# Second product of each attention score over 128 rows instead of 64, in a two-layer hybrid encoder

## The chip, the cores and the metric

The kernel runs on one core of a Trainium2 chip. The metric is device time in microseconds (us) of one execution; less is better. The engines of the core are PE (TensorE, the matrix engine; PEld is its loading of stationary operands), DVE (VectorE), ACT (ScalarE), POOL (GpSimd) and SP (SyncE, which here only issues transfers). They run unsynchronised, each through its own list of instructions, and wait for each other by semaphores.

## The reference

Two layers over 256 tokens of width 1024, in float32. Cut to what matters:

```python
h = rmsnorm(x, n1)
qa, ka, va, qb, kb, vb = jnp.split(h @ w_in, cuts, axis=-1)
ya = global_gqa(axial_rope(rmsnorm(qa)), axial_rope(rmsnorm(ka)), va)   # 8 heads, 2 k/v heads
yb = dilated_window_attention(partial_rope(qb), partial_rope(kb), vb)   # 8 heads
y = jnp.concatenate([rmsnorm(ya, out_norm_a), rmsnorm(yb, out_norm_b)], axis=-1)
x = x + y @ w_out
u = jnp.square(jax.nn.relu(rmsnorm(x, n2) @ w_mlp_in))
x = x + u @ w_mlp_out
```

Each of the 16 heads of a layer has 64 dimensions, so a score is a product over 64 rows: `s = q . k` for 256 queries and 256 keys, then a softmax and a product with v.

## The kernel before, in words

Every float32 operand of a product is held as two parts, hi (rounded to the type fp32r in which PE takes it) and lo (the rest), and a product is hi·hi + hi·lo + lo·hi. For the weights that is three products per block of 128 x 128, each of 256 columns (`block`). The weights come by DMA into `wraw`, ACT or DVE copies the hi part to `whi`, DVE or POOL subtracts to get `wlo`; all three are circular buffers that run ahead of PE.

A score uses the 128 rows of PE in another way. `q_split` puts a head's q into the tile `QS[i]` with the hi part on the head's 64 rows `a` and the lo part on the other 64 rows `b`. `k_split` puts k's hi part on both halves of `KA[i][0]` (in the B heads: of `KBt`), and k's lo part on the rows `a` alone of `KA[i][1]`. So `score` needs two products for each half `th` of the queries: one over 128 rows (q's hi and lo with k's hi) and one over 64 rows (q's hi with k's lo):

```python
for th in range(2):
    mm(b[:, th], q[:, th * 128:(th + 1) * 128], ks[0], True, False)
    mm(b[:, th], q[a, th * 128:(th + 1) * 128], ks[1][a], False, True)
```

In the trace these are the matmuls `bank<-ka,qs` and `bank<-kbt,qs`, and the form tells the rows: `128*128 128x256` or `64*128 64x256`. A head goes on from there: its row maxima on DVE (tile `hst`; for B heads with the mask, tile `pr`), the exponential on ACT (`pr`), the reciprocal of the sums on DVE (`hst`), the scaling of `pr` on POOL, DVE or ACT, four transposes on PE (`bank<-idt,pr`), their split into `h` (ACT) and `l` (DVE), and four products with V on PE (`bank<-h,V` and `bank<-l,V`, `pv`). A pair of heads then gives `yt`, split into `yA_` or `hh` and `hl`. Between the heads stand products that do not need them: q and k of the B heads (`fill_pair`, `bank<-hh,whi` and the like) and the output projection of the A heads (`fill_wa`, `bank<-yA_,whi`).

The order on each engine is made by `Sequencer`, a list schedule that knows data dependences and a table of costs; the cost of a matmul there depends on its columns and not on its rows. The order is fixed when the kernel is built. In the trace every instruction has line 368, that of `issue`, so groups are told apart by tiles.

Of the kernel before, what the change touches and what calls it, by code (L numbers as in the profile page):

```python
# [10 lines left out]
F32 = mybir.dt.float32  # L11
# [8 lines left out]
NRAW = 4096     # columns of weights as they come  # L20
NHI = 8192      # and split
# [6 lines left out]
NIN0 = 3                              # pairs of ff blocks in the K-outer start of the MLP  # L28
LAG = 2
N_PAIR = 16  # L30
# what an engine's end counts more, in the choice among several, per kind of instruction
# [3 lines left out]
def plan():  # L35
    """The weights in chunks of some columns, in the order in which TensorE takes them."""
    out = []
    for l in range(L):
        out += [(("A", l, kb), 640) for kb in range(8)]
        out += [(("V", l, kb), 640) for kb in range(8)]  # L40
        out += [(("B", l, p, i), 1024) for p in range(4) for i in range(2)]
        out += [(("WA", l, i), 1024) for i in range(4)]
        out += [(("WB", l, p), 1024) for p in range(4)]
        out += [(("IK", l, kb), 256 * NIN0) for kb in range(8)]
        for p in range(NIN0, N_PAIR):
            out += [(("IN", l, p, f), 1024) for f in range(2)]
            first = 0 if p == NIN0 else p - LAG
            out += [(("OUT", l, q, f), 1024) for q in range(first, p - LAG + 1) for f in range(2)]
        out += [(("OUT", l, p, f), 1024) for p in range(N_PAIR - LAG, N_PAIR) for f in range(2)]
    return out  # L50


def lay_weights(w_in, w_out, w1, w2):
    """The weights as TensorE takes them: rows of 128 on the partitions, columns
    in the heads' order (kv0 with kv1, first with second of a pair)."""
    def rows(w, idx, cols):
        return np.concatenate([w[i * 128:(i + 1) * 128][:, cols] for i in idx], axis=1)

    qcols = np.concatenate([np.concatenate([np.arange(64) + 64 * b, np.arange(64) + 64 * (b + 4)])
                            for b in range(4)])  # L60
    acols = np.concatenate([np.arange(512, 640), qcols])
    va, qb, kb, vb = 640, 768, 1280, 1792
    even = np.concatenate([np.arange(64) + va] + [np.arange(64) + vb + 64 * h for h in (0, 2, 4, 6)])
    odd = np.concatenate([np.arange(64) + va + 64] + [np.arange(64) + vb + 64 * h for h in (1, 3, 5, 7)])
    vcols = np.concatenate([even, odd])
    parts = []
    for (name, l, g, *i), n in plan():
        if name == "A":
            c = rows(w_in[l], (g,), acols)
        elif name == "V":  # L70
            c = rows(w_in[l], (g,), vcols)
        elif name == "B":
            c = rows(w_in[l], range(8), np.arange(128) + (qb, kb)[i[0]] + 128 * g)
        elif name == "WA":
            wa = w_out[l][qcols]
            c = np.concatenate([rows(wa, range(4), np.arange(128) + 128 * j) for j in (2 * g, 2 * g + 1)], axis=1)
        elif name == "WB":
            c = rows(w_out[l][512:], (g,), np.arange(1024))
        elif name == "IK":
            c = rows(w1[l], (g,), np.arange(256 * NIN0))  # L80
        elif name == "IN":
            c = rows(w1[l], range(8), np.arange(128) + 128 * (2 * g + i[0]))
        else:
            c = rows(w2[l], (2 * g + i[0],), np.arange(1024))
        assert c.shape == (128, n), (name, c.shape, n)
        parts.append(c.reshape(-1))
    return np.concatenate(parts)
# [20 lines left out]
def tables():  # L108
    """Constants that depend on shapes alone: rotary cosines and signed sines on
    [dim of two heads, token], the logarithms (times 8) of how many of the dilated  # L110
    patterns a key is in, the identity, and sums over a head or all."""
    f = np.float32
# [23 lines left out]
class Sequencer:  # L136
    """Takes a kernel's instructions in program order, keeps what that order says
    of their data, and issues them in the order of a list schedule: each engine takes,
    of what is ready for it, what has the longest way to the end."""

    # from the end of one engine's instruction to the start of another's that waits for it
# [20 lines left out]
    @staticmethod  # L162
    def form(e, method, args, kw):
        """An engine's instruction for what several engines can do."""
        if method == "copy":
            return ("activation", (*args, AF.Copy), {}) if e == "ACT" else ("tensor_copy", args, {})
        if method == "scale":
            o, a, f = args
            if e == "ACT":
                return "activation", (o, a, AF.Copy), {"scale": f}  # L170
            if e == "DVE":
                return "tensor_scalar", (o, a, f, None), {"op0": ALU.mult}
            return "tensor_scalar", (o, a, f, 1.0), {"op0": ALU.mult, "op1": ALU.mult}
        return method, args, kw

    @staticmethod
    def regions(ap, psum):
        """Where an access lies: partitions and spans of the free axis (a whole PSUM bank)."""
# [41 lines left out]
    def record(self, engines, method, args, kw):  # L220
# [28 lines left out]
        if engines == ("SP",):  # L249
            # the loads in program order  # L250
# [3 lines left out]
        # the SBUF port that DVE and Pool share  # L254
# [6 lines left out]
    def order(self):  # L261
# [31 lines left out]
        while done < n:  # L293
# [10 lines left out]
            if len(ops[i][0]) > 1:  # L304
                # the engine that ends it first
# [20 lines left out]
    def justify(self, start, end, succ):  # L326
        """Moves all instructions as late as they may be, then as early: gaps close."""
# [3 lines left out]
        for back in (True, False):  # L331
            busy = {e: [] for e in (*self.eng, "PORT")}     # spans, counted from this pass's beginning
# [28 lines left out]
    def issue(self):  # L361
        # once with the shared port, for the choice of engines, and once without
# [17 lines left out]
def trunk(ctx: ExitStack, tc: tile.TileContext, x, wts, prm, tab, fin, out):  # L380
# [19 lines left out]
    # ---------------------------------------------------------------- tiles  # L400
# [21 lines left out]
    KA = [[T(f"ka{i}{s}", [128, S], F32R) for s in range(2)] for i in range(2)]  # L422
# [3 lines left out]
    tq = T("tq", [128, 2, S])             # gain-folded sines of q and k  # L426
    tb = T("tb", [128, 2, S])             # rs-folded tables of B
# [16 lines left out]
    # ------------------------------------------------------------- weights  # L444
# [6 lines left out]
    def places(total):  # L451
        """Each chunk's place in a circular buffer, and the last chunk that it overwrites."""
# [23 lines left out]
    def prep_piece():  # L476
        """Splits a piece of the next chunk, if its place is free."""
# [27 lines left out]
    def wgt(key, a, n, last=True):  # L505
        """(hi, lo) of n columns from a on in a chunk; with `last`, their last use."""
# [17 lines left out]
    # --------------------------------------------------------- small pieces  # L524
    def col(src, rhs, n, o):
        """o[token, th, n] <- column sums of src [128, 256] (weights rhs)."""
# [3 lines left out]
    def rowbc(c2, o):  # L530
        """o [128, 256] <- c2 [token, th] along the free axis on every partition."""
# [8 lines left out]
    def sums(l, ps):  # L540
        """From column sums of squares of x: mean square + eps, and its power -1/2."""
# [11 lines left out]
    # ---------------------------------------------------------------- start  # L553
    DVE.memset(ssx[:, 0:128], 0.0)
    # TensorE's clock rises while it waits for x
# [10 lines left out]
    DVE.memset(one, 1.0)  # L566
    x3 = x.rearrange("p (a b) -> p a b", a=KB)
# [46 lines left out]
    def norm_x(l):  # L614
        """norm's scale along the tokens, from the squares' sums."""
# [8 lines left out]
    # ---------------------------------------------------------------- layer  # L624
    for l in range(L):
        gA, gA2, gK, gK2 = P(l, 16), P(l, 17), P(l, 18), P(l, 19)
        # gain-folded tables
# [3 lines left out]
        # ---- q and k of A, K-outer behind the split of h  # L631
# [7 lines left out]
        # ---- V of all heads, tokens on the partitions, with the rest of A's q, k between  # L639
# [17 lines left out]
        def k_split(kh, kst_):  # L657
            """kst_[head][hi, lo]: each a head's 64 rows twice."""
# [15 lines left out]
        cq = cqt.rearrange("p (t h) -> p t h", t=2)   # scale of q's scores / 8  # L674
# [78 lines left out]
        # ---- attention of the 16 heads, with the products that don't need it between  # L753
# [31 lines left out]
        def heads(k):  # L785
            """stationary q, moving k (hi, lo) and the V pair of head k of 16."""
# [6 lines left out]
        def score(k):  # L793
            q, ks, _ = heads(k)
            a = slice(64 * (k % 2), 64 * (k % 2) + 64)
            b = v2(bank[k % 2])
            for th in range(2):
                mm(b[:, th], q[:, th * 128:(th + 1) * 128], ks[0], True, False)
                mm(b[:, th], q[a, th * 128:(th + 1) * 128], ks[1][a], False, True)
# [40 lines left out]
        def pv(k):  # L840
# [10 lines left out]
            # rows of hi and lo parts together: a pair's y^T  # L851
# [77 lines left out]
        # ---- residual, norm2, MLP  # L929
# [37 lines left out]
        def mlp_out_t(ps_, banks=None):  # L967
            """W2 stationary: out^T."""
# [9 lines left out]
        # the last product's sums: half of the tokens, columns, bank  # L978
        outs = ((0, 0, 512, 1), (0, 512, 1024, 5), (1, 0, 512, 6), (1, 512, 768, 7), (1, 768, 1024, 4))

        def mlp_out_n(ps_, which=outs):
            """u^T stationary: out with tokens on the partitions."""
# [19 lines left out]
        def seed():  # L1002
            """The sums of the last product start from x, turned back."""
# [74 lines left out]
```

## Time and profile before

| what | value |
|---|---|
| median of 3 runs | 632.05 us |
| the three runs | 629.9, 632.05, 635.52 us |
| span of the profiled execution, first to last instruction | 630.3 us |
| busy share of the span: PE, DVE, ACT, POOL | 97%, 77%, 56%, 29% |
| mean granted clock of TensorE | 0.992 of full speed |

The profiled execution has its span as its own time; it lies 1.75 us under the median and inside the spread of the three runs. A busy share is a mean over stages. The attention of the first layer stands at about 45 to 128 us of the span, that of the second at 345 to 435 us; between and behind them lie the MLPs, where PE takes one matmul after another.

### The profile page before, as it was taken

The page shows a single profiled execution, that of the slowest core. Times are in us where ns is not written, and L with a number is a line of the kernel's source. Part 1 is how long each engine was busy: PE and PEld are TensorE (multiplying, and loading weights), DVE is VectorE, ACT ScalarE, POOL GpSimd, SP SyncE. Part 2 cuts the span into 40 slices and gives each one's busy share as a digit, 9 for nine tenths or more (in the row PEclk, how much of TensorE's full clock was granted, in tenths as well). Part 3 has the DMA queues.
Part 4 walks back from the last instruction along what each step waited for, and adds up shares of the span by engine and source line. Part 5 has one row for each costly group of instructions (what it writes and reads, how often), then busy time and mean ns, then how long its engine had stood idle before and what let it go on. Part 6 is the DMA issues. An engine that isn't in the chain of part 4 may idle for free.

```text
span 630.3 us, 11899 instructions
## 1 busy us (share of the span) xinstructions
PE 611.6 (97%) x4500; PEld 576.6 (91%) x4500; DVE 483.9 (77%) x873; ACT 353.4 (56%) x723; POOL 181.9 (29%) x179
## 2 busy tenths in 40 slices
PE   8989999989999999999999999999999999999996
PEld 8988987989999999999999888898989999999995
DVE  6898899998986566666588879887988766667632
ACT  6567877865544444434464687786654444434412
POOL 1486885841000000000035766667300000000000
PEclk9979999999999999999999999999999999999999
DMA  7833111346674554645444301025568554544501
GB/s 262 275 150 134 68 68 34 130 139 201 251 251 167 203 186 151 222 177 178 141 151 134 135 35 68 34 74 173 158 242 297 204 205 156 221 180 149 186 1 67
DMA packets 29865, 98.58 MB, mean 156 GB/s; under 512 B 3440, under 2 KB 3952, under 8 KB 29808
## 3 DMA queue, kind: packets, MB, share of 16 engines
q1 hardware_dynamic: 29808, 97.82, 44.3%
q8 instruction: 35, 0.57, 0.3%
q14 instruction: 22, 0.18, 0.1%
HBM read 96.76 MB, written 1.05 MB: 155 GB/s over the span
## 4 chain that ended last, share of the span: by engine, by line
PE 65%; DVE 11%; issue 2%; ACT 1%; POOL 1%; POOLq 0%; ACTq 0%; DVEq 0%
PE bank L368 65%; DVE wlo L368 2%; DVE f L368 2%; DVE hl L368 2%; DVE qs L368 1%; DVE hst L368 1%; DVE xT L368 1%; DVE l L368 1%; DVE pr L368 1%; DVE kbt L368 0%; POOL sm L368 0%; ACT f L368 0%; ACT pr L368 0%; POOL f L368 0%; DVE yA__82 L368 0%
## 5 line engine op out<-in xcount | busy, mean ns | idle before, releaser
L368 ACT ACTIVATE whi<-wraw 128x640 fp32r<-128x640 f32 (+3 forms) x312 | 192.9, 643 | 171.3 <-PE bank L368 113.0
L368 DVE TENSOR_TENSOR wlo<-wraw,whi 128x640 fp32r<-128x640 f32 (+3 forms) x296 | 221.0, 777 | 64.7 <-ACT whi L368 63.5
L368 PE MATMUL bank<-hh,whi 128*128 128x256 f32 x784 | 222.4, 285 | 0.7 <-ACT whi L368 0.7
L368 PE MATMUL bank<-hl,whi 128*128 128x256 f32 x784 | 222.5, 285 | 0.6 <-DVE hl L368 0.5
L368 PE MATMUL bank<-hh,wlo 128*128 128x256 f32 x784 | 221.2, 285 | 0.1
L368 PEld LDWEIGHTS bank<-hh,whi 128*128 128x128 f32 x784 | 149.2, 191 | 2.4 <-ACT whi L368 1.2
L368 PEld LDWEIGHTS bank<-hl,whi 128*128 128x128 f32 x784 | 148.1, 189 | 1.4 <-DVE hl L368 1.2
L368 PEld LDWEIGHTS bank<-hh,wlo 128*128 128x128 f32 x784 | 147.3, 189 | 0.6 <-DVE wlo L368 0.3
L368 POOL TENSOR_TENSOR wlo<-wraw,whi 128x384 fp32r<-128x384 f32 (+1 forms) x49 | 66.8, 1375 | 161.1 <-DMA wraw<-in_w_dram 149.7
L368 PE MATMUL bank<-l,whi 128*128 128x256 f32 x256 | 72.4, 283 | 0.0
L368 PE MATMUL bank<-h,wlo 128*128 128x256 f32 x256 | 72.2, 282 | 0.0
L368 PE MATMUL bank<-h,whi 128*128 128x256 f32 x256 | 71.3, 280 | 0.0
L368 POOL TENSOR_TENSOR sm<-sm,mhalf 128x2 f32<-128x2 f32 (+2 forms) x12 | 11.8, 986 | 183.8 <-DVE sm L368 183.8
L368 PE MATMUL bank<-wlo,h 128*128 128x512 f32 (+1 forms) x160 | 56.1, 350 | 0.0
L368 PE MATMUL bank<-whi,l 128*128 128x512 f32 (+1 forms) x160 | 55.9, 349 | 0.0
L368 PE MATMUL bank<-whi,h 128*128 128x512 f32 (+1 forms) x160 | 55.8, 349 | 0.0
L368 PEld LDWEIGHTS bank<-h,whi 128*128 128x128 f32 x256 | 48.4, 190 | 0.0
L368 PEld LDWEIGHTS bank<-h,wlo 128*128 128x128 f32 x256 | 48.0, 188 | 0.0
L368 PEld LDWEIGHTS bank<-l,whi 128*128 128x128 f32 x256 | 47.9, 187 | 0.1
L368 POOL TENSOR_TENSOR ssx<-ssx,f 128x512 f32<-128x512 f32 (+1 forms) x22 | 27.6, 1253 | 48.7 <-ACT f L368 37.3
L368 ACT ACTIVATE h<-f 128x512 fp32r<-128x512 f32 x32 | 20.2, 631 | 28.1 <-DVE f L368 28.1
L368 DVE CAST whi<-wraw 128x640 fp32r<-128x640 f32 (+1 forms) x33 | 14.8, 452 | 26.9 <-PE bank L368 25.6
(113 smaller groups left out, 994.8 us busy)
## 6 DMA issues: line engine op xcount, KB each, us to landing
wraw<-in_w_dram SPq DMA_DIRECT2D x148, 512.0 KB, 3.7
wraw<-in_w_dram SPq DMA_DIRECT2D x31, 320.0 KB, 3.3
wraw<-in_w_dram SPq DMA_DIRECT2D x16, 384.0 KB, 3.3
tabt<-in_t_dram SPq DMA_DIRECT2D x1, 768.0 KB, 7.5
xT<-in_x_dram SPq DMA_DIRECT2D x1, 512.0 KB, 7.0
tabt<-in_f_dram SPq DMA_DIRECT2D x1, 512.0 KB, 7.0
out_dram<-f SPq DMA_DIRECT2D x1, 512.0 KB, 2.6
out_dram<-f SPq DMA_DIRECT2D x2, 256.0 KB, 2.2
```

The costliest lines, as they stand in the source:

```text
L368: getattr(self.eng[e], method)(*args, **kw)
```

## The change

The second product runs over all 128 rows: the same stationary q (hi on the rows `a`, lo on `b`), with a moving operand that holds k's lo part on `a` and zeros on `b`. For that the four tiles of `KA` become slices of one tile `KAt`, so that the zero halves of `KAt` and `KBt` can be written once, at the start, by four memsets on POOL. `k_split` writes only the rows `a` of the lo tiles, so the zeros stay. The diff also drops comments and docstrings, which moves line numbers by a few and nothing else.

```diff
-    KA = [[T(f"ka{i}{s}", [128, S], F32R) for s in range(2)] for i in range(2)]
+    KAt = T("ka", [128, 2, 2, S], F32R)
+    KA = [[KAt[:, i, s] for s in range(2)] for i in range(2)]
...
     DVE.memset(one, 1.0)
+
+    for i in range(2):
+        b = slice(64 - 64 * i, 128 - 64 * i)
+        POOL.memset(KAt[b, i, 1].bitcast(F32), 0.0)
+        POOL.memset(KBt[b, :, i, 1].bitcast(F32), 0.0)
...
         q, ks, _ = heads(k)
-        a = slice(64 * (k % 2), 64 * (k % 2) + 64)
         b = v2(bank[k % 2])
         for th in range(2):
-                mm(b[:, th], q[:, th * 128:(th + 1) * 128], ks[0], True, False)
-                mm(b[:, th], q[a, th * 128:(th + 1) * 128], ks[1][a], False, True)
+                for s in range(2):
+                    mm(b[:, th], q[:, th * 128:(th + 1) * 128], ks[s], s == 0, s == 1)
```

On POOL, at the start of the program (`ssx` are the sums of squares of x, `f_98` a scratch tile that was `f_101` before, since three tiles fewer are numbered), this stands after the change:

```order
L368 IOTA idt 128x128
L368 MEMSET ka 64x256
L368 MEMSET kbt 64x3x256 x2
L368 MEMSET ka 64x256
L368 TENSOR_TENSOR ssx<-ssx,f_98 128x512 x3
L368 TENSOR_TENSOR ssx<-ssx 128x256
```

The four memsets are new, between the identity's iota and the first sum of squares; the rest of POOL's list is as before.

On PE, at the first two scores of layer 1 (`ka_85` and `ka_86` are hi and lo of the first k head, `ka_87` and `ka_88` of the second, `bank_63` and `bank_64` the scores' banks), this stood before:

```order
L368 MATMUL bank_67<-whi,hl 128x320
L368 MATMUL bank_63<-ka_85,qs_83 128x256
L368 MATMUL bank_63<-ka_86,qs_83 128x256
L368 MATMUL bank_63<-ka_85,qs_83 128x256
L368 MATMUL bank_63<-ka_86,qs_83 128x256
L368 MATMUL bank_64<-ka_87,qs_84 128x256
L368 MATMUL bank_64<-ka_88,qs_84 128x256
L368 MATMUL bank_64<-ka_87,qs_84 128x256
L368 MATMUL bank_64<-ka_88,qs_84 128x256
L368 MATMUL bank_68<-hh,whi 128x256
```

And this stands there now:

```order
L368 MATMUL bank_67<-whi,hl 128x320
L368 MATMUL bank_63<-ka,qs_83 128x256 x4
L368 MATMUL bank_64<-ka,qs_84 128x256 x4
L368 MATMUL bank_68<-hh,whi 128x256
L368 MATMUL bank_68<-hl,whi 128x256
```

Nothing moved: the same eight matmuls stand at the same place and read as two rows because they now have one tile. But for the four memsets, every engine has the same instructions in the same order with the same waits as before.

## Rows read from the trace of the kernel before

**Rows 1.** Stretches: length, busy PE, PEld, DVE, ACT, POOL (instructions), granted clock.

```profile
45.00:128.00 83.00, 80.99 (x574) 71.75 (x572) 76.01 (x163) 66.37 (x169) 62.47 (x65) 1.00 0.27 95
150.00:300.00 150.00, 150.00 (x1252) 149.86 (x1251) 106.05 (x172) 67.31 (x112) 0.71 (x1) 1.00 0.56 198
345.00:435.00 90.00, 88.02 (x619) 78.37 (x619) 76.05 (x168) 70.44 (x180) 62.84 (x65) 1.00 0.23 77
```

**Rows 2.** Timeline, first two scores: start us, us, engine, operation, out<-in, count.

```profile
46.26 2.46 PE L368 MATMUL bank<-ka,qs 128*128 128x256 f32 x8
48.65 0.39 PE L368 MATMUL bank<-hh,whi 128*128 128x256 f32 x1
48.87 0.28 PE L368 MATMUL bank<-hl,whi 128*128 128x256 f32 x1
48.87 0.19 PEld L368 LDWEIGHTS bank<-hh,wlo 128*128 128x128 f32 x1
```

**Rows 3.** Timeline of PE, products with V: one stationary operand, one bank.

```profile
102.71 0.28 PE L368 MATMUL bank<-h,V 128*128 128x256 f32 x1
102.83 0.28 PE L368 MATMUL bank<-l,V 128*128 128x256 f32 x1
```

**Rows 4.** Matmuls that read ka in the whole run, with their forms.

```profile
L368 PE MATMUL bank<-ka,qs x64: 279/382/386, 46.3 to 377.3; 128*128 128x256 f32 x32, 64*128 64x256 f32 x32
```

**Rows 5.** What DVE waited for in 45 to 128 us: total, times, longest.

```profile
DVE hst L368 <- PE bank L368: 2.5, 4, 0.7
DVE l L368 <- ACT h L368: 1.0, 3, 0.4
DVE hst L368 <- ACT pr L368: 0.8, 2, 0.4
DVE pr L368 <- PE bank L368: 0.5, 2, 0.3
DVE f L368 <- PE bank L368: 0.3, 1, 0.3
```

**Rows 6.** Chain that ended last, its PE pieces in 345 to 435 us.

```profile
356.53 21.19 PE bank L368 x140
404.47 3.15 PE bank L368 x18
410.16 24.42 PE bank L368 x191
```

**Rows 7.** Score matmuls in these three pieces, with their forms.

```profile
L368 PE MATMUL bank<-ka,qs x24: 279/382/386, 356.5 to 377.3; 128*128 128x256 f32 x12, 64*128 64x256 f32 x12
L368 PE MATMUL bank<-kbt,qs x4: 381/382/385, 404.5 to 405.8; 128*128 128x256 f32 x2, 64*128 64x256 f32 x2
L368 PE MATMUL bank<-kbt,qs x7: 378/383/384, 411.6 to 413.6; 64*128 64x256 f32 x4, 128*128 128x256 f32 x3
```

**Rows 8.** What DVE waited for PE alone in 345 to 435 us.

```profile
DVE hst L368 <- PE bank L368: 3.0, 5, 1.5
DVE pr L368 <- PE bank L368: 0.6, 1, 0.6
```

**Rows 9.** Timeline of PE after two long waits; then a stretch's clock (third figure).

```profile
36.66 1.64 PE L368 MATMUL bank<-idt,f 128*128 128x2 f32 x8 [2.10 <-DVE f L368]
129.72 0.43 PE L368 MATMUL bank<-idt,sm 128*128 128x128 f32 x2 [1.60 <-POOL sm L368]
36.90:43.70 6.80, 6.80 (x29) 0.50 0.24 81
```

**Rows 10.** Timeline of POOL at the start, and a scaling by it.

```profile
9.84 1.33 POOL L368 TENSOR_TENSOR ssx<-ssx,f 128x512 f32<-128x512 f32 x1 [8.77 <-ACT f L368]
99.64 0.48 POOL L368 TENSOR_SCALAR pr<-pr,hst 128x256 f32<-128x256 f32 x1 [0.71 <-DVE hst L368]
```

**Rows 11.** Timeline of DVE, one operation at two places.

```profile
102.91 1.75 DVE L368 TENSOR_TENSOR qs<-f,qs 64x256 fp32r<-64x256 f32 x1
110.08 0.42 DVE L368 TENSOR_TENSOR qs<-f,qs 64x256 fp32r<-64x256 f32 x1
```

## The prediction, made before the run

> **What bounds the kernel now.** I read first the busy time by stage, then PE's timeline at the scores, then what DVE waits for in the two attention stretches and the chain that ended last, and at the end the places where PE stood idle.
>
> In the MLP stretch from 150 to 300 us PE is never idle and DVE is busy for 106 us of 150 [rows 1]: PE alone sets the time there, at 150 / 1252 = 0.120 us from one matmul of mostly 256 columns to the next. The change touches nothing in it. In the attention stretches two engines are full: PE shows 80.99 of 83 us in layer 1 and 88.02 of 90 in layer 2, DVE 76.01 and 76.05 [rows 1]. A busy PE there is not a PE at its pace. From 45 to 128 us it starts 574 matmuls, which at 0.120 us (the 320-column ones and transposes set against each other) is 69 us, not 83. The missing time is found at the scores. The first two scores are eight matmuls, four over 128 and four over 64 rows in turn; they start at 46.26 us, the next product at 48.65 and the one behind it at 48.87 [rows 2]. Nine matmuls took 2.61 us where nine of the MLP take 1.08. The excess is 1.53 us, or **0.38 us for each matmul over 64 rows**: about 0.19 at the step from 128 rows to 64 and as much at the step back.
>
> So the question is not whether PE gains, but how much of the gain DVE lets through.
>
> **The change part by part.** *The 64-row products become 128-row products.* There are 32 of them on `ka` [rows 4], and as many on `kbt`, since the A and the B heads are eight each in both layers: 64 in all, 32 in each layer. After the change no matmul of the score has another number of rows than its neighbours. Does the excess then go? The nearest rows are the products with V: `h` and `l` follow each other with the same stationary operand into the same bank, as the two products of a score will, and stand 0.12 us apart [rows 3]. So I count the full 0.38 for each: 12.2 us of PE's time in each layer, 24.4 in all. The other bound is no gain at all on PE; it is a rival below.
>
> *What of it reaches the end, layer 1.* DVE's instructions, their order and what they wait for stay as they are, so DVE can come forward only by the time in which it waits for something that PE releases. From 45 to 128 us it is idle for 83 − 76.01 = 7.0 us, of which the larger waits make 5.1 [rows 5]. The 0.8 us for ACT's `pr` are not PE's: DVE gives the maximum, ACT takes the exponential, DVE waits for its sums. What is left is at most 2.5 + 1.0 + 0.5 + 0.3 = **4.3 us**; what PE releases directly is 2.5 + 0.5 + 0.3 = **3.3 us**. (The waits for ACT's `h` come from PE's transposes, but these also wait for the scaled `pr`.) PE's 12.2 us cover either. The rest, 12.2 less 3.3 to 4.3, turns into waits of PE for `l`, `qs`, `kbt`, `hl` from DVE: what is late next is DVE's list.
>
> *Layer 2.* Here the chain that ended last passes through PE in three pieces, of 21.19, 3.15 and 24.42 us, and between them through DVE, which stands back to back [rows 6]. In these pieces lie 12, 2 and 4 matmuls over 64 rows [rows 7]; 18 x 0.38 = **6.8 us** is the most by which this chain can shorten, the other 14 lie where DVE sets the pace. What DVE waits for PE directly at the scores is 3.0 + 0.6 = **3.6 us** [rows 8]; that is the lower bound.
>
> *The four memsets.* POOL has nothing to do until 9.84 us, after a wait of 8.77 us [rows 10]. The trace has no memset of this size; the nearest row, a scaling of 128x256 at 0.48 us [rows 10], gives 0.48 + 0.48 for the two of 256 columns and twice three times that for the two of 768, 3.8 us, from about 1.1 to 5 us. The wait for the squares covers it. If it collided with DVE's first work at 4 to 5 us, it could push that by one such memset at most, 1.4 us; less than nothing it cannot cost, since nothing goes away on POOL. I take 0. The merging of the four `KA` tiles into one adds no wait on any engine and costs 0.
>
> *The sum.* Layer 1 gives 3.3 to 4.3, layer 2 gives 3.6 to 6.8: together 6.9 to 11.1. The upper end needs every wait to go and no new round trip between two full engines, the lower end that nothing behind ACT is gained. I take the middle, **9.0 us**, since neither excludes the other. The profiled execution of 630.3 us would become 621.3; set against the median of the three runs, 632.05, it is **623.0 us** (rounded down from 623.05). One per cent is 6.3 us, about what a measurement of this kernel can tell from no change (the three runs lie 5.6 us apart).
>
> **The rivals.** *DVE closes all its gaps.* If the short waits, below what the view names, go as well and all of layer 2's idle time is used, DVE comes forward by 83 − 76.01 = 7.0 us in layer 1, and in layer 2 PE's 12.2 us bind before DVE's 90 − 76.05 = 13.95. Together 19.2 us: 612.8 us. For it: the idle time is there, and DVE's own instructions are not all as short as they can be: the same subtraction for `qs` took 1.75 us at one place and 0.42 at another [rows 11], so another timing against POOL could shorten some. Against it: part of the idle time is the small gap behind each of 163 and 168 instructions, and the chain of layer 2 allows 6.8. PE's full 24.4 us (607.6 us) would need DVE to do 76.01 us of work in 70.8, which only shorter DVE instructions could bring.
>
> *The excess is not of the rows.* If 0.3 us is the price of loading q twice in a row, or of two products into one half of a bank, the second product stays as dear, and the time stays at 632. Against it stand the products with V [rows 3]; for it, that no row shows two 128-row score products behind each other. The Trainium skill has a rule that points this way: "TensorE: Matmul & The Clock Gate", Part 3 (The mechanism), says that a weight load overlaps running matmuls only when the row group differs. By that rule two loads over all 128 rows would stand one behind the other after the change too, and nothing would be gained. The trace does not bear it out: the load for `hh,wlo` starts at 48.87 us, with the start of the 128-row matmul ahead of it [rows 2]. The same section's other way out, a background weight buffer, fits the row better.
>
> *The slower one: PE's clock.* Layer 1 shows the mechanism before the attention. PE stood idle for 2.10 us until 36.66, and then ran from 36.9 to 43.7 us at a granted clock of 0.50, which is the lower level of 1.2 GHz; a wait of 1.60 us until 129.72 had no such effect, the stretches around it are at 1.00 [rows 9, 1]. PE's new waits in the attention are 24.4 − 9.0 = 15.4 us. Over 32 heads that is 0.5 us each, and then nothing happens. If they gather in a few places of 2 us and more, above all at the norm behind each attention, where 1.60 us is there already, each fall takes half of 6.8 us, 3.4 us of PE's work. From three falls (10.2 us) on the gain is eaten, provided that they lie where PE is needed, as it is behind the norm; five would give 632.05 − 9.0 + 17 = 640 us.
>
> **How the numbers follow.** The forecast (DVE lets 6.9 to 11.1 us through, a little more or less where DVE and POOL collide otherwise) has 0.68. Closing most of DVE's gaps, 613 to 617 us, has 0.14. No gain, 632 us, has 0.10: one kind of row speaks clearly against it. The clock has 0.05, since it needs several long waits; 0.03 is left for what I do not see. The range begins at 612, the end of the first rival with a little play. It ends at 629.5: the lower bound of the forecast is 625.1, and some 4 us more are for the memsets' 1.4, for one fall of the clock, or for collisions. It leaves out no gain, most of the clock and the rest, and so holds about 0.8. Faster by over 1% is under 625.7: about five sixths of the forecast's 0.68 and all of the first rival's 0.14, 0.72 with a little off for the spread of the runs. Within 1%: the rest of the forecast, no gain, and a single fall of the clock, 0.23. Slower by over 1%: 0.05, the clock and the unseen.
>
> **What the profile after would show.** The row-switch is right if all score matmuls stand 0.12 us apart and have one form, and if the eight of the first two scores take about 1 us instead of 2.4. The bound is right if DVE's waits for PE at `hst`, `pr` and `f` nearly go, while PE's waits for DVE in the attention grow from under 2 us to more than 5 us in each layer, and the stretch of layer 1 ends some 4 us earlier, that of layer 2 some 9 us. The MLP stretches must keep their length. The forecast fails low if DVE's own instructions get shorter or if DVE had more hidden waits than the view names; it fails high if PE's granted clock shows 0.50 in or behind an attention, or if the score matmuls stay 0.3 us apart.

## The result, and the profile after

The changed kernel took 623.74 us (median of 4 runs, 622.36 to 625.17), the kernel before beside it 630.98 us: a ratio of 0.9863, 95% interval [0.9828, 0.9897]. A second measurement of the same kernel gave 623.11 us and 0.9857 [0.9826, 0.9887]. The prediction was 623.0 us.

One thing is needed to read the times below. Each run lists its mean granted clock, and a run's time goes with it: the 67 runs of the kernel before that list it have a median of 632.7 us, the 24 of them at a mean clock of 0.994 to 0.997 one of 630.8 us, the 5 below 0.985 one of 637.8 us. Where a time is called "at equal clock" it is the median of the runs at 0.994 to 0.997. The changed kernel has 622.6 us there (4 runs), so the change is worth 8.2 us at equal clock (a difference of two medians, without an interval).

The profiled execution of the changed kernel spans 620.6 us against 630.3. Where the 9.7 us lie is told by two marks: the first row maximum of each attention on DVE (tile `hst`; in layer 2 the products `bank<-idt,sm` some 7 us ahead of it) and PE's products `bank<-idt,sm` of the norm behind the attention. The stretches between these marks, from the view of stretches (columns as in [rows 1]); first the kernel before:

```profile
47.51:129.72 82.21, 78.60 (x560) 69.78 (x560) 75.19 (x164) 64.89 (x166) 61.36 (x66) 1.00 0.28 95
347.02:433.46 86.44, 84.46 (x593) 75.02 (x593) 73.73 (x164) 68.12 (x175) 60.18 (x63) 1.00 0.23 80
```

And the same stretches of the changed kernel, with a piece of its MLP:

```profile
46.80:125.64 78.84, 68.94 (x543) 65.08 (x542) 75.29 (x164) 63.20 (x164) 61.18 (x66) 1.00 0.30 99
342.95:423.91 80.96, 74.24 (x593) 71.56 (x593) 74.80 (x164) 67.57 (x175) 60.48 (x63) 1.00 0.27 83
150.00:300.00 150.00, 150.00 (x1251) 149.86 (x1250) 106.71 (x171) 66.72 (x110) 1.56 (x1) 1.00 0.58 197
```

Layer 1 is 3.4 us shorter, layer 2 5.5 us, and 0.7 us were won before the first mark; there the stretch at the lower clock of [rows 9] was half as long in this execution (PE ran at 0.50 from 37.6 to 41.0 us, and at 1.00 from 41.1 us on), which is not the change's: it was as short in the kernel before with more matmuls (below; 3.4 us from 38.7 us on), and the kernel with the zeros alone had none there. It also shortened layer 1's own stretch, so that the 3.4 us are too much by more than 1 us (the first experiment). The MLP between them is as long as it was: 347.02 − 129.72 = 217.30 us before, 342.95 − 125.64 = 217.31 us after, PE full as in [rows 1]. In the attentions DVE's busy time has hardly moved (75.19 and 73.73 before, 75.29 and 74.80 after, the same 164 instructions), but the stretch around it has closed in: DVE's idle time went from 7.0 to 3.6 us and from 12.7 to 6.2 us. PE's busy time fell by 9.7 and 10.2 us, 19.9 in all (of layer 1's part some 2 us are 17 matmuls that PE had behind it at the first mark, 543 against 560); its idle time grew by 6.3 and 4.7 us, 11.0 in all; the difference is the 8.9 us by which the stretches are shorter.

The timeline of PE at the first two scores answers [rows 2]:

```profile
44.12 1.11 PE L368 MATMUL bank<-ka,qs 128*128 128x256 f32 x8
45.07 0.28 PE L368 MATMUL bank<-hh,whi 128*128 128x256 f32 x1
```

Eight matmuls from 44.12 to 45.07: 0.95 us where 2.39 us stood, 0.119 us each. In the whole run they now have one form, and a median of 283 ns instead of 382 [rows 4]; the view of tile `ka` also shows the weight loads and the memsets (minimum, median, maximum in ns):

```profile
L368 PEld LDWEIGHTS bank<-ka,qs x64: 186/190/247, 44.0 to 369.1; 128*128 128x128 f32 x64
L368 PE MATMUL bank<-ka,qs x64: 277/283/387, 44.1 to 369.2; 128*128 128x256 f32 x64
...
L368 POOL MEMSET ka<- x2: 304/305/306, 1.1 to 2.9; 64x256 f32 x2
```

What DVE waited for, 45 to 124 us (answers [rows 5]); then, 342 to 424 us, what it waited for PE alone ([rows 8]):

```profile
DVE hst L368 <- ACT pr L368: 0.8, 2, 0.4
DVE l L368 <- ACT h L368: 0.8, 2, 0.5
DVE yt L368 <- ACT f L368: 0.2, 1, 0.2
...
DVE f L368 <- PE bank L368: 0.2, 1, 0.2
DVE pr L368 <- PE bank L368: 0.2, 1, 0.2
DVE hst L368 <- PE bank L368: 0.2, 1, 0.2
```

In layer 1 no wait of DVE for PE is left in the view (3.3 us before), in layer 2 there are 0.6 us (between the same marks 3.8 before: the 3.6 of [rows 8] and 0.2 for `f`). What came in their place are waits of PE. The same view for PE, first of the kernel before (45 to 128 and 345 to 435 us), then of the changed one:

```profile
PE bank L368 <- DVE l L368: 1.4, 2, 1.2
...
PE bank L368 <- DVE l L368: 1.7, 3, 1.2
```

```profile
PE bank L368 <- DVE l L368: 5.1, 5, 1.9
PE bank L368 <- ACT pr L368: 1.4, 1, 1.4
PE bank L368 <- POOL ssx L368: 0.7, 1, 0.7
...
PE bank L368 <- DVE l L368: 3.0, 3, 1.7
PE bank L368 <- ACT pr L368: 1.8, 1, 1.8
PE bank L368 <- ACT h L368: 1.4, 3, 0.5
```

PE now waits longest for `l`, the lo part of the probabilities that DVE subtracts. The chain that ended last shows the same turn in layer 2: the long pieces of PE in [rows 6], 21.19, 3.15 and 24.42 us, have become these, with short pieces of DVE, ACT and PE between them:

```profile
352.45 5.58 PE bank L368 x45
...
390.66 3.40 PE bank L368 x27
...
396.44 2.79 PE bank L368 x18
...
408.92 16.11 PE bank L368 x133
```

### The profile page after: what moved, and what is told of

Its sections match the earlier page's. It is cut to its first block, busy times and chain, and to the rows that moved or that the text cites. A ratio compares the mean times of both kernels' runs of the same rounds, so it can differ in the third digit from the quotient of the medians.

```text
span 620.6 us, 11904 instructions
## 1 busy us (share of the span) xinstructions
PE 591.7 (95%) x4500; PEld 569.0 (92%) x4500; DVE 484.8 (78%) x873; ACT 352.4 (57%) x723; POOL 186.0 (30%) x183
## 4 chain that ended last, share of the span: by engine, by line
PE 64%; DVE 12%; issue 1%; ACT 1%; POOL 0%; POOLq 0%; ACTq 0%; DVEq 0%
PE bank L368 64%; DVE wlo L368 2%; DVE f L368 2%; DVE hl L368 2%; DVE hst L368 1%; DVE qs L368 1%; DVE l L368 1%; DVE xT L368 1%; ACT pr L368 1%; DVE kbt L368 1%; DVE pr L368 1%; DVE yt L368 1%; ACT f L368 0%; POOL sm L368 0%; DVE yA__82 L368 0%
## 5 line engine op out<-in xcount | busy, mean ns | idle before, releaser
L368 POOL TENSOR_TENSOR ssx<-ssx,f 128x512 f32<-128x512 f32 (+1 forms) x22 | 29.0, 1320 | 45.7 <-ACT f L368 35.0
```

Of the source, the lines that this page charges most:

```text
L368: getattr(self.eng[e], method)(*args, **kw)
```

## The experiments

**The zeros without the longer product.** The changed kernel with its merged tile and its memsets, but the second product over 64 rows again:

```diff
-                for s in range(2):
-                    mm(b[:, th], q[:, th * 128:(th + 1) * 128], ks[s], s == 0, s == 1)
+                mm(b[:, th], q[:, th * 128:(th + 1) * 128], ks[0], True, False)
+                mm(b[:, th], q[a, th * 128:(th + 1) * 128], ks[1][a], False, True)
```

> The merged k tile and the four memsets as in the change, the second product still over 64 rows. Theory (the whole gain comes from the row switches): the time of the kernel before, 631 us, within 2 us; score matmuls 0.31 us apart as before; attention stretches as long as before. Rival (the memsets or the merged tile shift the start, which gives part of the gain, since the changed kernel reached its first score 2.1 us earlier): 629 us or less, and the first score as early as in the changed kernel.

Measured 631.88 us, ratio 0.9992 [0.9972, 1.0013]; at equal clock 631.0 against 630.8 us. The tile and the memsets cost nothing that can be measured, and all of the gain is the longer product's. Half of the rival's sign came true all the same: the first score started at 42.45 us, earlier than in the changed kernel, and the time did not follow. In this profile PE ran at the full clock ahead of layer 1, and the stretch of layer 1 is shorter without the change. Its row, and what DVE waited for the scores in 45 to 127 us:

```profile
46.67:127.59 80.92, 75.91 (x543) 67.41 (x543) 75.04 (x164) 63.75 (x164) 61.40 (x66) 1.00 0.29 97
...
DVE hst L368 <- PE bank L368: 1.2, 2, 0.6
```

PE has the same 543 matmuls in it as in the changed kernel; the kernel before has 560, and waits of DVE for scores of 2.5 us [rows 5], because PE came to the first scores late, out of the long stretch at the lower clock. Against this row layer 1's gain is 80.92 − 78.84 = 2.1 us and not 3.4. In layer 2 the clock fell in this execution, at 398.2 us, though from 390 us on PE shows a single wait, of 0.19 us (timeline, then the stretch's clock):

```profile
395.57 0.38 PE L368 MATMUL bank<-l,V 128*128 128x256 f32 x1 [0.19 <-DVE l L368]
...
398.20:405.00 6.80, 6.80 (x27) 5.91 (x28) 5.59 (x17) 3.02 (x11) 4.40 (x5) 0.50 0.00 0
```

**Only the A heads, only the B heads.** `r` is all 128 rows for one kind of head and the head's 64 for the other:

```diff
+            r = slice(0, 128) if k < 8 else slice(64 * (k % 2), 64 * (k % 2) + 64)
...
+                mm(b[:, th], q[r, th * 128:(th + 1) * 128], ks[1][r], False, True)
```

> The A heads' second product over 128 rows, the B heads' over 64: half of the row switches go. Theory (only what DVE waits for passes): DVE's waits for PE lie mostly in the A half (3.3 of 4.3 us in layer 1, 12 of the 18 matmuls on the chain in layer 2), so this half brings about 6 to 7 us: 624 to 625 us. Rival (the gain is the same for each switch that goes): half of 7.2 to 9.7 us, 626 to 627 us.

> The reverse: B heads over 128 rows, A heads over 64. Theory: 1.5 to 3 us of gain, 628 to 629.5 us, since DVE is back to back in most of the B half. Rival (the same for each switch): 626 to 627 us.

The A heads alone (`k < 8`) gave 629.88 us, 0.9964 [0.9943, 0.9984]: a miss. The B heads alone gave 628.8 us, 0.9947 [0.9922, 0.9971], inside what was expected, but not for the reason given. In layer 2, where neither profile has a stretch at a lower clock, the attention (first with the A heads, then with the B heads) took 83.53 and 83.86 us, 2.9 and 2.6 us less than before:

```profile
347.93:431.46 83.53, 79.20 (x594) 73.22 (x593) 74.93 (x164) 68.07 (x175) 60.55 (x63) 1.00 0.26 82
...
344.94:428.80 83.86, 79.46 (x593) 73.33 (x593) 73.58 (x164) 67.73 (x175) 60.43 (x63) 1.00 0.26 81
```

The two kinds of heads are worth the same there, and together the 5.5 us of the whole change. At equal clock the B heads have 627.3 us (5 runs), 3.5 us less than the kernel before and again near half of 8.2: the expected inequality is out, and the rival (the same for each change of rows) is nearer. A part of the first kernel's miss is the clock. Its runs have a median clock of 0.9875 (the kernel before 0.992), and its one run at 0.995 took 627.06 us, 3.7 us less than the kernel before. Timeline of PE in its layer 1, then two stretches there (granted clock third from the end):

```profile
50.04 0.80 PE L368 MATMUL bank<-ka,qs 128*128 128x256 f32 x2 [2.83 <-ACT pr L368]
...
88.04 0.61 PE L368 MATMUL bank<-idt,ssx 128*128 128x1 f32 x4 [0.70 <-POOL ssx L368]
```

```profile
49.00:55.80 6.80, 5.76 (x27) 5.76 (x28) 5.80 (x12) 4.77 (x14) 4.37 (x5) 0.51 0.28 109
...
90.00:96.80 6.80, 6.80 (x28) 5.90 (x29) 6.08 (x17) 5.09 (x16) 4.31 (x5) 0.50 0.01 4
```

Twice in an attention the granted clock was at half, the level of 1.2 GHz: once from within a wait of 2.83 us for ACT's `pr` on, once from 2 us behind a wait of 0.70 us and some short matmuls on. This is the prediction's slower rival, in a kernel with half of the change. It is not the change's alone: the zeros alone had such a fall too, if more seldom (their runs have a median clock of 0.9945).

**Half of the switches.** The kernel before, with both 128-row products of a score first and both 64-row products behind them (only the first product then opens the bank; in the changed kernel both halves open it, so that is not where the price lies):

```diff
-            for th in range(2):
-                mm(b[:, th], q[:, th * 128:(th + 1) * 128], ks[0], True, False)
-                mm(b[:, th], q[a, th * 128:(th + 1) * 128], ks[1][a], False, True)
+            for th in range(2):
+                mm(b[:, th], q[:, th * 128:(th + 1) * 128], ks[0], th == 0, False)
+            for th in range(2):
+                mm(b[:, th], q[a, th * 128:(th + 1) * 128], ks[1][a], False, True)
```

> The kernel before with another order in a score: both 128-row products first, then both 64-row products, so that four row switches a head become two; same rows, same loads. Theory (the price is for a switch, 0.19 us, and none for 64 rows as such): the two 64-row products stand 0.12 us apart, PE saves 12 of 24 us, and 5 to 8 us of it reach the end: 623 to 626 us. Rival (a 64-row product is dear by itself, or a second load of the same q is): no gain, 631 us.

Measured 625.46 us, 0.9898 [0.9874, 0.9922]. The timeline of its first two scores; the second line is the first pair of 64-row products, from a view of that pair alone:

```profile
42.15 1.69 PE L368 MATMUL bank<-ka,qs 128*128 128x256 f32 x8
42.48 0.50 PE L368 MATMUL bank<-ka,qs 64*128 64x256 f32 x2
43.77 0.39 PE L368 MATMUL bank<-hh,whi 128*128 128x256 f32 x1
43.99 0.28 PE L368 MATMUL bank<-hl,whi 128*128 128x256 f32 x1
```

Nine starts take 43.99 − 42.15 = 1.84 us; less 9 x 0.12 that is 0.76 us too much, half of the 1.53 of the kernel before, for the same four 64-row products and half as many changes of the row count. So a change costs 0.19 us. One thing that was expected is missed: the two 64-row products do not stand 0.12 us apart but 0.22 (the pair lasts 0.50 us, its second product 0.28). The two 128-row products behind the last change stand 43.99 − 43.77 = 0.22 us apart as well. The price of a change thus falls on two starts, some 0.1 us on each; by the starts in the trace the first of them is 0.21 us in either direction, and for the 64 rows themselves nothing is left. No run has three 64-row products in a row. This halves PE's saving to 12.2 us, and yet by the ratios 6.4 us are won (0.0102 x 631), where the full change has 8.6 to 9.0: the second half of PE's saving brings little (how little is open, since the intervals of the two ratios overlap).

**PE's work put back, in both kernels.** Each first product of a score is issued three times instead of once, with the order of all else kept: 128 more matmuls of 0.12 us, 15.4 us of PE's work, and nothing more for any other engine.

```diff
+            if method == "matmul" and kw["start"] and not kw["stop"] and "qs" in args[1].tensor.name:
+                for _ in range(2):
+                    self.eng[e].matmul(*args, **kw)
```

> The changed kernel, with each score's first 128-row product issued three times instead of once: two further products per half of a score, 128 in all, the order of all else kept; each starts its bank anew, so the sums stay what they are. At the 0.12 us that a product of this shape takes in the changed kernel's rows this is 15.4 us of TensorE work (7.7 us a layer), with no further work on any other engine. Theory (after the change VectorE carries the attention, 95% and 92% busy there, and TensorE waits for it some 16 us a layer): most of the 15.4 us lies in TensorE's waits, at most 3 to 4 us come through, 623 to 627 us. Rival (TensorE still sets the attention's end, and the change was worth 7 to 9 us because most of the 24 us never was there): all of it comes through, 638 us, six or more above the kernel before.

> The same two further 128-row products per half of a score in the kernel before: 15.4 us of TensorE work more, the 64-row second product kept. Theory (in the kernel before TensorE bounds more of the attention than VectorE: VectorE idle 7.0 us in layer 1 and 12.7 us in layer 2, TensorE only 3.6 and 2.0 us): more of it comes through than in the changed kernel, 8 to 13 us, so 640 to 645 us against 632 us. Rival (the share that comes through is the same in both kernels, as it would be if the gain of the change came from something else than a shift of the bound from TensorE to VectorE): 633 to 636 us if it is small in both, 647 us if it is whole in both.

The changed kernel went to 626.29 us, at equal clock 626.4: 3.8 of the 15.4 us came through. The kernel before went to 641.5 us, 1.0131 [1.0069, 1.0194], at equal clock 641.8: 11.0 of the 15.4 us. Both are as the theory had it, and both rivals are out: neither does all of the work come through in the changed kernel, nor the same share in both. The stretches of the attentions, the changed kernel with the products first:

```profile
46.70:125.96 79.26, 73.89 (x607) 72.03 (x606) 75.17 (x164) 63.68 (x164) 61.35 (x66) 1.00 0.30 98
343.48:427.91 84.43, 80.36 (x657) 78.70 (x657) 75.48 (x164) 67.81 (x175) 60.24 (x63) 1.00 0.26 79
```

```profile
47.38:134.66 87.28, 84.51 (x617) 76.12 (x616) 74.63 (x164) 63.87 (x164) 60.29 (x66) 1.00 0.28 89
351.75:443.38 91.63, 91.29 (x657) 82.34 (x657) 73.81 (x164) 67.78 (x175) 59.53 (x63) 1.00 0.23 74
```

DVE's work is one number in all four stretches of each layer, some 75 and 74 to 75 us. In layer 1 of the changed kernel 7.7 us of PE's work cost 0.4 us, because DVE needs 75 of 79 us whatever PE does; in layer 2 they cost 3.5. In the kernel before they cost 5.1 and 5.2 us, and its layer 2 then has PE busy for 91.29 of 91.63 us, with DVE waiting for PE's scores for `hst` and `pr` (the three added lines make `issue` line 371):

```profile
DVE hst L371 <- PE bank L371: 6.8, 6, 2.0
...
DVE pr L371 <- PE bank L371: 2.7, 3, 1.3
```

**A lighter DVE under both row counts.** The subtraction that makes `l` is left out, and the product with V uses `h` twice (so the probabilities' lo part is missing), once with 64-row and once with 128-row second products; the orders are planned anew.

```diff
-            DVE.tensor_tensor(out=lo, in0=tk, in1=h.bitcast(F32), op=ALU.subtract)
-            PT[k] = (v2(h), v2(lo))
+            PT[k] = (v2(h), v2(h))
```

> Less work on DVE in the attention, score as before the change (second product over 64 rows): the lo part of the transposed weights of the softmax is left out, so DVE's 32 subtractions for l (0.69 us each, 22 us in all) go, and the products with V take h twice, so that PE's work stays. It is only to be compared with e6_light_128, which differs by the rows alone. Theory (PE sets the pace here): a few us under the kernel before, 622 to 630 us. Rival (DVE sets the pace already before the change): 12 us or more under it.

> The same with less work on DVE, and the second product over 128 rows. Theory (the change gives PE 24.4 us, and DVE's list is what kept all but 9 of it from the end): with 11 us less on DVE in each layer much more passes, 15 to 22 us between e5_light_64 and this one. Rival (what keeps the gain back is a round trip or the clock, not DVE's load, or PE never gained 24 us): the difference stays at 7 to 10 us.

They took 628.88 us, 0.9935 [0.9905, 0.9964], as expected, and 614.81 us, 0.9725 [0.9694, 0.9755]: the row count is worth 14.1 us here (13.1 at equal clock, with a single run at 128 rows), against 8.2 us with the full DVE. That lies between the theory's 15 to 22 and the rival's 7 to 10, nearer to the theory. Stretches of the second kernel, and what its PE waited for in layer 2:

```profile
46.21:119.72 73.51, 66.97 (x534) 64.92 (x533) 67.24 (x155) 63.23 (x162) 54.34 (x62) 0.98 0.31 100
337.54:414.27 76.73, 73.35 (x595) 71.17 (x593) 69.26 (x155) 66.48 (x171) 58.38 (x63) 1.00 0.30 97
```

```profile
PE bank L368 <- ACT pr L368: 1.6, 1, 1.6
PE bank L368 <- POOL pr L368: 0.8, 2, 0.6
```

With `l` gone PE waits for the exponential and its scaling. DVE does carry the attention, but with it lighter by 8 and 5.5 us ACT, at 63 and 66 us, stands close behind.

**Three tries for a better version.** First, V's hi and lo as stationary operands of their own, so that PE adds a pair of heads and ACT and DVE are spared copies and sums (12 instead of 8 products with V for a pair):

```diff
-                w = V2[:, kb, i, vi, :]
-                mm(o, w, h[:, kb], kb == 0, False)
-                mm(o, w, lo[:, kb], False, kb == 1)
+                vh, vl = (w[:, kb, vi, 64 * i:64 * i + 128] for w in (VH, VL))
+                mm(o, vh, h[:, kb], kb == 0 and i == 0, False)
+                mm(o, vh, lo[:, kb], False, False)
+                mm(o, vl, h[:, kb], False, kb == 1 and i == 1)
```

> A version for use, from the changed kernel: v's hi and lo parts lie in separate stationary operands with zeros in the other head's half, so that PE itself sums a pair's hi and lo products into one result. It adds 2 matmuls of 0.12 us a head (3.8 us of PE in each layer), and takes from DVE two additions a pair (6.9 us in each layer) and from ACT one copy of two. Theory (DVE bounds the attention after the change, PE has room): 6 to 12 us under the changed kernel, 612 to 618 us. Rival (PE or a round trip bounds it): no gain or up to 7 us slower, 623 to 631 us.

It took 632.48 us, 0.9990 [0.9958, 1.0023]: failed. Then the planner's number for GpSimd, from −700 to −1000 and to −400 (`PEN`, the first entry):

> The changed kernel, with the planner's malus on GpSimd for general pieces raised from 700 to 1000 in favour of it (POOL -1000): of the pieces that subtract the weights' high parts 88 instead of 49 lie on GpSimd and 257 instead of 296 on VectorE; all engines' orders are planned anew. Theory (VectorE bounds the attention after the change, so work taken off it is time won, unless GpSimd's pieces slow VectorE's by sharing its way to the memory): VectorE is relieved of 39 pieces, 1 to 4 us won, 619 to 622 us. Rival (GpSimd's pieces make VectorE's neighbours longer, as its 64x256 subtraction took 1.75 us instead of 0.42 us in the kernel before, so that the relief is given back, or the new order loses it): 623 to 629 us.

> The changed kernel with the planner's number for GpSimd at -400 instead of -700: 23 instead of 49 of the subtractions of weights lie on GpSimd and 322 instead of 296 on VectorE; orders planned anew. Theory (VectorE's work bounds the attention): 26 more pieces on VectorE cost 1 to 4 us, 624 to 627 us. Rival (VectorE is slowed by GpSimd beside it more than by the work that it would take over): 617 to 622 us.

They took 630.49 us, 0.9953 [0.9914, 0.9991], and 631.14 us, 0.9980 [0.9944, 1.0015], both slower than the changed kernel. All three are slower than either of the ranges that were expected for them. All three have new orders, and in all three profiles the clock fell in the attentions, so they don't tell much of the pieces themselves. The rows that still do, the attention of layer 2 of the first and of the second, and a stretch of the second's layer 1:

```profile
343.83:432.84 89.01, 79.90 (x625) 78.08 (x625) 79.55 (x160) 65.79 (x164) 67.12 (x70) 0.96 0.34 108
```

```profile
351.21:431.21 80.00, 75.44 (x594) 71.69 (x593) 69.22 (x160) 67.26 (x173) 69.04 (x71) 1.00 0.29 93
...
106.50:109.90 3.40, 3.40 (x17) 3.40 (x18) 2.85 (x9) 1.28 (x3) 1.69 (x3) 0.54 0.02 6
```

The first has four instructions less on DVE and yet 4.8 us more of DVE time, since more of the weights' subtractions came to lie in this stretch (by the groups 17 of them instead of 8, 19.0 us instead of 9.2). The second is the one undisturbed stretch: 5.6 us less on DVE and 8.6 us more on POOL than in the changed kernel made it 1.0 us shorter. How such an order would do without the falls of the clock stays open.

## Why the prediction was right

*PE's saving.* The prediction counted 0.38 us for each 64-row product, 0.19 per change of rows, and took the products with V [rows 3] as the pattern for what remains. The changed kernel shows 0.119 us, and the experiment with half of the changes gives 0.19 us for each. The rival "the excess is not of the rows" is out. In the changed kernel each load of a stationary q takes 190 ns and the matmuls start 119 ns apart, so 128-row loads do overlap 128-row matmuls. The rule in the Trainium skill, "TensorE: Matmul & The Clock Gate", Part 3 (The mechanism), that a load overlaps only when the row group differs, does not hold here. Another of its pages, "TensorEngine Tiling (Array Packing)", Key Properties, says that a change of the tiling mode drains TensorE, without a price; the 0.19 us agree with it.

*What DVE lets through.* Foretold were 3.3 to 4.3 us in layer 1 and 3.6 to 6.8 in layer 2, 9.0 in all; the profile shows 3.4 and 5.5, 8.9 in all, and the runs at equal clock 8.2. The agreement in layer 1 is luck. Its 3.3 us were read in an execution in which the lower clock had made PE late for the first scores; in the profile of the zeros alone DVE's direct waits for PE are 1.2 + 0.5 + 0.3 = 2.0 us, and against it the change is worth 2.1. So layer 1's term was too large by 1.2 us or more, and 2.1 and 5.5 us make 7.6. That the time came within 0.7 us of the forecast is in part luck too: the forecast set out from 632.05 us, and the four runs beside the change have 630.98. The attentions end 4.1 and 9.6 us earlier, where some 4 and 9 were foretold; the same luck is in both, since the zeros alone end layer 1 at 127.59 us, 2.1 us earlier than the kernel before. In layer 2 the mechanism is seen whole. DVE's idle time fell by 6.5 us (its waits from 347 to 434 us before, from 342 to 424 after): 3.2 in its waits for PE (3.8 to 0.6), 1.6 in those for ACT's `h` (2.5 to 0.9), 1.0 for ACT's `f` (3.0 to 2.0) and 0.7 for POOL's `sm` (0.7 to none); DVE's work took 1.1 us more, and 5.5 are left. So waits behind ACT shrank too, which the lower end of 3.6 us had left out. PE's waits in the view rose from 1.9 in each layer to 7.8 and 6.8 us; for DVE alone they are 5.5 and 3.6 us, so the mark of 5 was missed in layer 2, where ACT's `pr` and `h` took DVE's place. Of the 24.4 us, 11.0 are idle time of PE in the view and 8.9 are won. Where the rest went is seen in layer 2 by the starts of PE's matmuls in the trace: against the closest spacing of each shape they lag by 20.7 us in the stretch before and by 15.2 after, of which the view calls 2.0 and 6.7 idle. The others lie under the modelled end of the matmul before, which lasts 0.28 us where the next can start after 0.12. So of layer 2's 12.2 us 5.5 were won, 4.7 became idle time in the view and 2.0 waits too short for it. The saturation is measured: from the kernel before, 15.4 us of PE's work more cost 11.0 us, 12.2 us less bring 6.4, and the second 12.2 less bring some 2.

*The place of it in layer 2* was argued wrongly. Of the 18 matmuls in the chain's PE pieces 12 belong to A heads [rows 7], so the A heads should have brought twice what the B heads bring; they brought 2.9 and 2.6 us. The chain names one path of one execution. That PE's scores are close behind it where it runs through DVE would explain the equal halves, but is not shown.

*The memsets* took 0.31 us for 256 columns and 0.73 and 0.82 for 768, where 0.48 and 1.44 were estimated from a scaling. From the view of tile `kbt`, then the timeline of POOL (answers [rows 10]):

```profile
L368 POOL MEMSET kbt<- x2: 731/774/818, 1.4 to 2.2; 64x768 f32 x2
...
1.37 1.60 POOL L368 MEMSET kbt<- 64x768 f32 x2
2.92 0.30 POOL L368 MEMSET ka<- 64x256 f32 x1
10.55 1.30 POOL L368 TENSOR_TENSOR ssx<-ssx,f 128x512 f32<-128x512 f32 x1 [7.33 <-ACT f L368]
```

They end at 3.22 us, 7.33 us before POOL's next work: cost 0, as taken.

*The rivals on the other side.* DVE did not close all its gaps, 3.6 and 6.2 us are left; nor did its instructions get shorter: the subtraction for `qs` that took 1.75 us [rows 11] took 1.75 us again. The clock did not fall in an attention in the two profiles of the changed kernel. But the condition that the prediction set for it, waits of 2 us and more, was wrong: the A heads alone had one of its two falls behind a wait of 0.70 us, and the zeros alone one with hardly a wait ahead of it.

## What to carry to other kernels

Before a product is cut to fewer rows, look at its neighbours: with a spacing of 0.12 us between matmuls of one row count and 0.31 where the count changes each time, rows of zeros were cheaper than none, and already sorting the products by row count brought most of it. Work taken off the busiest engine is worth what the second one lets pass, and the idle time of that second engine, less its waits that others release, was a fair measure of it, if the execution in which it is read was not late for another reason, as it was here by a stretch at the lower clock; putting the work back and adding more gives the whole curve. In a kernel in which PE waits often, compare runs at the same granted clock, since the spread by the clock (630.8 to 637.8 us here for one kernel) is as large as the gain.

## What the runs showed of the hardware

A change between 128 and 64 rows costs PE 0.19 us at 256 columns, in both directions, and delays the next two starts by some 0.1 us each: 0.21 and 0.22 us in place of 0.12. The second product behind a change starts after 0.22 us whether it has 64 or 128 rows. With 128 rows throughout, loads of 190 ns each go beside matmuls that start every 119 ns. The granted clock fell to 0.50 in attentions in which PE had idled once for 2.83 us, once for 0.70 us with short matmuls around it, and once not longer than 0.19 us from 390 to 398 us, while waits of 1.4 to 1.9 us in the changed kernel had no such effect: one wait's length alone does not tell it. A memset of zeros by GpSimd took 0.31 us for 64 x 256 elements in float32 and 0.73 and 0.82 us for 64 x 768.
